# Normalising the sparse-attention probabilities inside the product that transposes them

## The chip, the cores and the metric

The kernel runs on one core of one Trainium2 chip. The metric is the device time of one launch in microseconds; the time before is the median of three runs. A core has a TensorE (PE, its weight loads shown apart as PEld), a VectorE (DVE), a ScalarE (ACT), a GpSimd (POOL) and a SyncE (SP). Each takes its own instructions in order; they wait for each other through semaphores.

## The reference, cut to what matters

Two transformer blocks follow one another on 512 tokens of width 1024. The change lies in the second block, in its sparse attention (16 heads, head size 64), whose two branches, "selected blocks" and "window", are both dense causal softmax attention at this length:

```python
s_s = jnp.einsum('bqghd,bgqkd->bgqhk', qb, k_g).astype(jnp.float32) * scale + group_bias(...)
p_s = masked_softmax(s_s, (dist_s >= 0)[:, :, :, None, :])
o_s = jnp.einsum('bgqhk,bgqkd->bqghd', p_s.astype(v_g.dtype), v_g)
...
out = gb[..., 0:1] * o_c + gb[..., 1:2] * o_s + gb[..., 2:3] * o_w
```

So each row of exponentials is divided by its sum and multiplied by a gate of the branch, and is then multiplied with the values.

## The kernel before

The kernel runs through block 1, then through a stage in which block 2 is projected, then through the stage `pa2` (opened in `emit`), then through the tail (mix, cross attention, feed-forward). In `pa2` three streams of work are woven by `weave`: the sparse attention (`nsa`, four groups of four heads, two branches each: 32 calls of `attend` with a gate), the RWKV recurrence (`rwkv_backs`, then `merge`, tiles with the suffix `_b` and `psn`) and a dense product for the gates (`merge_gates`, tiles `psg_m`). `attend` itself holds no yield, yet in the trace the instructions of the other streams stand between its own: the framework's planner lays out every engine's order when the kernel is compiled, by its own estimate of when each instruction is ready, and every engine then runs its list in that order.

One call of `attend` (L299 to L333) does this. For four blocks of 128 queries it multiplies queries with keys (L311, L312, into the PSUM tiles `psa`), adds the bias and takes the row minimum on DVE (L313), and takes the exponential and its row sum on ACT (L315). DVE takes the reciprocals of the four sums (L316) and multiplies them by the gate (L318). Then every probability tile is scaled in place by its row's reciprocal: the two wide ones (128x384 and 128x512) on ACT (L321), the two narrow ones on DVE (L323). After that, for four blocks of keys, PE transposes 4, 3, 2 and 1 squares of 128x128 (L328, ten in a call, into `psb`), ACT rounds the result (L330), DVE takes the remainder (L331), and two products with the values add up the output (L332, L333, into `pso`).

`attend` is called eight more times in block 1 without a gate. The transposes of a call are one instruction each: the moving operand is the identity, the stationary one is the probability square. The tile pool of `pa2` gives the key tiles (`kst`, pairs of high and low part) six buffers; `merge` later uses the same buffers for the operands of a product.

Of the kernel before, what the change touches and what calls it, by code (L numbers as in the profile page):

```python
# [11 lines left out]
AF = mybir.ActivationFunctionType  # L12
OP = mybir.AluOpType
# [25 lines left out]
class Gen:  # L39
# [259 lines left out]
    def attend(self, qst, kst, bias, V, o, first, last, gate=None):  # L299

        nc = self.nc
        kh, kl = kst
        st = self.f("sm", shape=(128, 32))
        m, s, r = st[:, 0:4], st[:, 4:8], st[:, 8:12]
        Pt = self.f("p", shape=(128, 1280))
        P = [Pt[:, 64 * i * (i + 1):64 * (i + 1) * (i + 2)] for i in range(4)]
        for i, pt in enumerate(P):
            w = 128 * (i + 1)
            ps = self.ps("a")
            qt = qst[:, i * 128:i * 128 + 128]  # L310
            nc.tensor.matmul(ps[:, :w], qt, kh[:, :w], start=True, stop=False)  # L311
            nc.tensor.matmul(ps[:, :w], qt, kl[:, :w], start=False, stop=True)  # L312
            nc.vector.tensor_tensor_reduce(pt, ps[:, :w], bias[:, 512 - w:], 1.0, 3e38, OP.add, OP.min,  # L313
                                           m[:, i:i + 1])
            nc.scalar.activation(pt, pt, AF.Exp, bias=m[:, i:i + 1], scale=-1.0, accum_out=s[:, i:i + 1])  # L315
        nc.vector.reciprocal(r, s)  # L316
        if gate is not None:
            nc.vector.tensor_tensor(r, r, gate, OP.mult)  # L318
        for i, pt in enumerate(P):
            if i >= 2:  # L320
                nc.scalar.activation(pt, pt, AF.Copy, scale=r[:, i:i + 1])  # L321
            else:
                nc.vector.tensor_scalar(pt, pt, r[:, i:i + 1], None, op0=OP.mult)  # L323
        for j in range(4):
            w = 512 - 128 * j
            ps = self.ps("b")
            for i in range(j, 4):
                nc.tensor.transpose(ps[:, (i - j) * 128:(i - j + 1) * 128], P[i][:, j * 128:j * 128 + 128], self.ident)  # L328
            ph, pl = self.f("pt", F32R), self.f("pt", F32R)
            nc.scalar.copy(ph[:, :w], ps[:, :w])  # L330
            nc.vector.tensor_tensor(pl[:, :w], ps[:, :w], ph[:, :w].bitcast(F32), OP.subtract)  # L331
            nc.tensor.matmul(o[:, j * 128:], V(j), ph[:, :w], start=first and j == 0, stop=False)  # L332
            nc.tensor.matmul(o[:, j * 128:], V(j), pl[:, :w], start=False, stop=last and j == 3)  # L333
# [903 lines left out]
    def merge(self, live):  # L1237

        nc, A, V = self.nc, self.A, self.nc.vector

        def first(n, g, p):
            self.mg.append(self.f("xh"))
            V.scalar_tensor_tensor(self.mg[n], g, 1.0, p, OP.add, OP.mult)

        def second(n, g, p):
            V.scalar_tensor_tensor(g, g, 1.0, p, OP.add, OP.mult)
            V.tensor_tensor(self.mg[n], self.mg[n], g, OP.add)

        def residual():
            x = self.x = [self.xtile(k, F32) for k in range(8)]  # L1250
            for k in range(8):
                nc.sync.dma_start(x[k], self.x2d[k])
            rs = self.bcast(self.colf)
            for k in range(8):
                V.scalar_tensor_tensor(x[k], x[k], self.vec("norm_final", k), rs, OP.mult, OP.mult)
                if "first" in self.dbg:
                    nc.sync.dma_start(self.dbg["first"][k * 128:(k + 1) * 128], x[k])
                yield 0.6
        while "_m" in live:
            yield None  # L1260
        self.mg = []
        load, product = self.branch(A["w_br_r"], self.yrd, 0, first,
                                    [("kb", 1024), ("y", 1024), ("vs", 1024), ("vu", 1024), ("bk", 1024), ("ys", 1024), ("as", 1024),
                                     ("y", 1024)], "vgb", "vgb")
        yield from load
        while "" in live and (w := next(product, None)) is not None:
            yield w
        while "" in live:
            yield None
        load, product_n = self.branch(A["w_br_n"], self.ynd, 8, second, ["kst"] * 3 + ["qst"] * 2 + ["pt"] * 2 + [("p", 1280)],  # L1270
                                      "f", "f")
        yield from self.side_by_side([product, load])
        yield from self.side_by_side([product_n, residual()])
# [169 lines left out]
def emit(tc, A, out, dbg={}):  # L1443
    nc = tc.nc
    with ExitStack() as ctx:
        g = Gen(tc, A, out, ctx)
        g.dbg = dbg
        scr = lambda n, s: setattr(g, n, nc.dram_tensor(n, s, F32, kind="Internal").ap())
        for n, s in dict(x2d=(8, 128, T), yrd=(8, 128, T), ynd=(8, 128, T), gtd=(128, T), gfd=(16, 1056),
                         grd=(16, 2, 640), adr=(4, 2, 4, 8, 32, 32), ydr=(4, 64, 32, 32), decd=(8, 128, 8), kbd=(8, 128, 1024),  # L1450
                         trd=(8, 128, 1024), tad=(8, 128, 1024), vgd=(8, 8, 128, T),
                         kvd=(8, 128, T), qd=(8, 128, T), vd=(2, 4, 128, 256), zmd=(16, 128, T),
                         ckd=(8, 128, 256), cvd=(2, 2, 128, T)).items():
            scr(n, s)
        g.setup()
        with g.phase("b1", act=16, f=3, sq=4, rs=3):
            xs = g.block1()
        g.banks = {"g": "01", "g_p": "23", "a": "45", "n": "6", "n_p": "7", "b": "67"}
        g.close_r()
        with g.phase("rec"):  # L1460
            g.rwkv_state()
            with g.phase("pa1", f=7, src_p=2, blk=2, cw=2, lt=3, kb=1, rkv=6, ar=1, cum=2, cx=1,
                         ys=1, f_p=4, cx_p=1, ws_p=2, wh_p=2, wl_p=2, **{"as": 1}):
                g.rwkv_consts()
                g.reserve(rkv=512, f=512, cum=520, cx=512, ar=1024, kb=1024, lt=1024, ys=1024, src_p=512, blk=1024,
                          cw=1024, cx_p=512, f_p=512, ws_p=1024, wh_p=1024, wl_p=1024, **{"as": 1024})
                g.run(g.rwkv_low(xs))

                def others():
                    yield from g.projections(xs)  # L1470
                    yield from g.merge_gates(xs, range(43, 49))
                g.weave(("", g.rwkv_fronts(xs), 245), ("_p", others(), 170))
            g.banks = {"a": "01", "b": "23", "n": "2", "o": "4", "a_b": "5", "b_b": "6", "g_m": "7", "g_b": "56"}
            g.side = nc.gpsimd
            with g.phase("pa2", f=3, ld=3, qst=5, kst=6, p=2, pt=4, bias=2, pc=2, kz=1, o=1, ot=1, vt=1,
                         kb=1, v=1, bk=1, ys=1, vs=2, vu=2, yc=6, vgb=2, y=2, f_m=1, **{"as": 1}):
                g.reserve(kb=1024, v=512, vs=1024, vu=1024, yc=128, bk=1024, y=1024, ys=1024,
                          vgb=512, ld=512, kst=512, vt=2048, qst=512, f=512, pc=512, bias=512)

                live = {"", "_m"}  # L1480

                def until(n, gen):
                    yield from gen
                    live.remove(n)

                def right():
                    yield from g.rwkv_backs()
                    yield from g.merge(live)
                g.weave(("", until("", g.nsa()), 190), ("_b", right(), 240), ("_m", until("_m", g.merge_gates(xs, range(49, 59))), 65))
            g.halves, g.side = None, nc.sync  # L1490
        g.banks = {"g": "01", "n": "2", "a": "34", "b": "56", "o": "7"}
        with g.phase("tail", act=52, f=16):
            g.mix()
            g.cross()
            g.ffn()
        g.close_r()
# [131 lines left out]
```

## Time and profile before

| what | us |
|---|---|
| median of three runs | 2083.45 (2080.49 to 2084.88) |
| profiled execution, its own time | 2082.19 |
| span of the profiled execution | 2080.4 |
| PE busy in the span | 2004.5 (96%) |
| DVE busy | 1308.6 (63%) |
| ACT busy | 925.3 (44%) |

The spans of the table are of one profiled execution; what lies around its span is 1.8 us. An instruction on PE is shown as a weight load (PEld) and a matmul; matmuls overlap each other, so a sum of their durations says more than the time that they cost, and the step from one start to the next is what counts. The 32 gated calls of `attend` lie between 1083 and 1450 us of the span.

### The profile page before, as it was taken

To read this page: it belongs to the slowest core of one execution; us is meant where nothing else is said; L and a number is where in the kernel's file an instruction comes from. 1 tells how busy PE (TensorE), PEld (TensorE's weight loads), DVE (VectorE), ACT (ScalarE), POOL (GpSimd) and SP (SyncE) were. 2 spreads that over 40 slices of the span, in tenths; PEclk is the share of its full clock that TensorE was granted. 3 is DMA by queue.
4 is the path that set the end of the run, shared out by engine and by line. 5 is a ranking of instruction groups with operands and counts; after the bars stand their busy time and mean duration, and the time that the engine had idled before them with its cause. 6 is when DMAs were issued, how large, how long until landed. Compare 5 with 4: busy or idle time off the path is not lost.

```text
span 2080.4 us, 27852 instructions
## 1 busy us (share of the span) xinstructions
PE 2004.5 (96%) x9927; PEld 1627.0 (78%) x9927; DVE 1308.6 (63%) x3007; ACT 925.3 (44%) x1778; POOL 95.5 (5%) x167
## 2 busy tenths in 40 slices
PE   8999999999999899899988899999999999999999
PEld 7778888888888677777767687887878778888887
DVE  5785432554463568687848988888466756666522
ACT  4874531442254233333346577777243443333311
POOL 0000000000003200000120111000000000000000
PEclk9999999999999999999989899999999999999999
DMA  5222332333355754755673445446442123333332
GB/s 161 82 85 93 99 93 92 117 108 120 117 185 158 171 147 141 183 147 168 191 168 105 129 122 145 126 123 190 154 140 84 41 81 92 101 92 98 95 109 84
DMA packets 178267, 256.75 MB, mean 123 GB/s; under 512 B 95409, under 2 KB 109953, under 8 KB 178129
## 3 DMA queue, kind: packets, MB, share of 16 engines
q1 hardware_dynamic: 162832, 231.31, 38.2%
q0 software_dynamic: 15296, 23.66, 3.9%
q8 instruction: 79, 1.29, 0.3%
q14 instruction: 60, 0.48, 0.1%
HBM read 205.12 MB, written 45.53 MB: 120 GB/s over the span
## 4 chain that ended last, share of the span: by engine, by line
PE 46%; DVE 6%; ACT 3%; issue 2%; DMA 2%; SPq 0%; POOL 0%; DVEq 0%; ACTq 0%; POOLq 0%
PE psg L243 8%; PE psg L245 8%; PE psg L244 8%; PE psg_b L243 1%; PE psg_b L244 1%; PE psg_b L245 1%; PE psb L328 1%; DVE ys L777 1%; PE psg_p L243 1%; PE psg_p L244 1%; PE psg_p L245 1%; PE pso L332 1%; PE psa L744 1%; DVE ys L778 1%; PE pso L333 1%
## 5 line engine op out<-in xcount | busy, mean ns | idle before, releaser
L222 ACT CAST wh<-ws 128x1024 fp32r<-128x1024 f32 (+2 forms) x283 | 291.6, 1031 | 697.9 <-PE psg L244 457.1
L223 DVE TENSOR_TENSOR wl<-ws,wh 128x1024 fp32r<-128x1024 f32 (+2 forms) x283 | 339.4, 1201 | 266.3 <-ACT wh L222 265.7
L243 PE MATMUL psg<-xh,wh 128*128 128x512 f32 x984 | 392.2, 399 | 4.7 <-ACT wh L222 4.7
L245 PE MATMUL psg<-xh,wl 128*128 128x512 f32 x984 | 393.1, 399 | 0.0
L244 PE MATMUL psg<-act,wh 128*128 128x512 f32 x912 | 359.7, 395 | 1.1 <-DVE act L166 1.1
L243 PEld LDWEIGHTS psg<-xh,wh 128*128 128x128 f32 x984 | 186.0, 189 | 46.8 <-ACT wh L222 5.5
L245 PEld LDWEIGHTS psg<-xh,wl 128*128 128x128 f32 x984 | 186.0, 189 | 41.5 <-issue 1.2
L244 PEld LDWEIGHTS psg<-act,wh 128*128 128x128 f32 x912 | 171.1, 188 | 42.8 <-DVE act L166 1.5
L243 PE MATMUL psg<-act,wh 128*128 128x512 f32 x496 | 196.1, 397 | 2.8 <-ACT act L165 1.4
L245 PE MATMUL psg<-act,wl 128*128 128x512 f32 x496 | 196.1, 396 | 0.5 <-DVE wl L223 0.5
L244 PE MATMUL psg<-xl,wh 128*128 128x512 f32 x352 | 139.7, 397 | 0.0
L243 PEld LDWEIGHTS psg<-act,wh 128*128 128x128 f32 x496 | 92.8, 188 | 27.2 <-ACT act L165 2.2
L245 PEld LDWEIGHTS psg<-act,wl 128*128 128x128 f32 x496 | 93.0, 187 | 23.7 <-DVE wl L223 1.3
L315 ACT ACTIVATE p<-p,sm 128x128 f32<-128x128 f32 (+3 forms) x160 | 89.6, 561 | 15.0 <-DVE sm L313 13.6
L331 DVE TENSOR_TENSOR pt<-psb,pt 128x512 fp32r<-128x512 f32 (+3 forms) x160 | 75.8, 487 | 20.0 <-ACT pt L330 17.7
L244 PE MATMUL psg<-x,wh 128*128 128x512 f32 x216 | 88.2, 409 | 0.0
L313 DVE CUSTOM_DVE_ANT_0 p<-psa,bias 128x128 f32<-128x128 f32 (+3 forms) x160 | 75.9, 485 | 8.2 <-PE psa L312 6.1
L328 PE MATMUL psb<-ident,p 128*128 128x128 f32 x400 | 75.3, 285 | 2.5 <-DVE y L921 0.9
L244 PEld LDWEIGHTS psg<-xl,wh 128*128 128x128 f32 x352 | 66.3, 188 | 14.0
L330 ACT CAST pt<-psb 128x512 fp32r<-128x512 f32 (+3 forms) x160 | 65.8, 424 | 25.7 <-PE psb L328 20.8
L243 PE MATMUL psg_p<-xh,wh 128*128 128x512 f32 x176 | 73.3, 416 | 1.1 <-ACT f L957 0.6
L244 PE MATMUL psg_p<-x,wh 128*128 128x512 f32 x176 | 72.2, 410 | 0.0
(491 smaller groups left out, 3899.1 us busy)
## 6 DMA issues: line engine op xcount, KB each, us to landing
ws<-in_w_in SPq DMA_DIRECT2D x49, 512.0 KB, 4.0
ws<-in_w_fup SPq DMA_DIRECT2D x44, 512.0 KB, 3.5
ws<-in_w_up SPq DMA_DIRECT2D x32, 512.0 KB, 3.5
ws<-in_w_down SPq DMA_DIRECT2D x32, 512.0 KB, 3.6
ws<-in_w_fdn SPq DMA_DIRECT2D x16, 512.0 KB, 3.6
ws<-in_w_qku SPq DMA_DIRECT2D x12, 512.0 KB, 3.6
ws<-in_w_in POOLq DMA_DIRECT2D x10, 512.0 KB, 4.6
ws<-in_w_out SPq DMA_DIRECT2D x8, 512.0 KB, 3.5
```

What stands on the lines that cost most here:

```text
L222: nc.scalar.copy(wh[:, :n], ws[:, :n])
L223: nc.vector.tensor_tensor(wl[:, :n], ws[:, :n], wh[:, :n].bitcast(F32), OP.subtract)
L243: nc.tensor.matmul(p[:, :n], wh[:, s], h[:, :n], start=c + k == 0, stop=False)
L244: nc.tensor.matmul(p[:, :n], wh[:, s], l[:, :n], start=False, stop=False)
L245: nc.tensor.matmul(p[:, :n], wl[:, s], h[:, :n], start=False, stop=last)
L313: nc.vector.tensor_tensor_reduce(pt, ps[:, :w], bias[:, 512 - w:], 1.0, 3e38, OP.add, OP.min, m[:, i:i + 1])
L315: nc.scalar.activation(pt, pt, AF.Exp, bias=m[:, i:i + 1], scale=-1.0, accum_out=s[:, i:i + 1])
L328: nc.tensor.transpose(ps[:, (i - j) * 128:(i - j + 1) * 128], P[i][:, j * 128:j * 128 + 128], self.ident)
L330: nc.scalar.copy(ph[:, :w], ps[:, :w])
L331: nc.vector.tensor_tensor(pl[:, :w], ps[:, :w], ph[:, :w].bitcast(F32), OP.subtract)
L332: nc.tensor.matmul(o[:, j * 128:], V(j), ph[:, :w], start=first and j == 0, stop=False)
L333: nc.tensor.matmul(o[:, j * 128:], V(j), pl[:, :w], start=False, stop=last and j == 3)
```

## The change

In gated calls the in-place scaling is dropped. Instead DVE builds, in one instruction, four diagonal squares in a new tile `dg` (128x512): the identity times the reciprocal of each row, once for each of the four query blocks. The transpose of a probability square is replaced by an ordinary fp32 matmul whose moving operand is the matching diagonal square. Calls without a gate keep the old form. To make room, `kst` has four buffers in `pa2` instead of six, and `dg` has two; `merge` takes a `dg` pair where it took the third `kst` pair.

```diff
-        for i, pt in enumerate(P):
-            if i >= 2:
-                nc.scalar.activation(pt, pt, AF.Copy, scale=r[:, i:i + 1])
-            else:
-                nc.vector.tensor_scalar(pt, pt, r[:, i:i + 1], None, op0=OP.mult)
+        if gate is not None:
+            dg = self.f("dg").rearrange("p (i n) -> p i n", i=4)
+            nc.vector.tensor_tensor(dg, self.ident[:, None, :].to_broadcast([128, 4, 128]),
+                                    r[:, :, None].to_broadcast([128, 4, 128]), OP.mult)
+        else:
+            dg = None
+            for i, pt in enumerate(P):
...
-                nc.tensor.transpose(ps[:, (i - j) * 128:(i - j + 1) * 128], P[i][:, j * 128:j * 128 + 128], self.ident)
+                src, dst = P[i][:, j * 128:j * 128 + 128], ps[:, (i - j) * 128:(i - j + 1) * 128]
+                if dg is not None:
+                    nc.tensor.matmul(dst, src, dg[:, i], start=True, stop=True)
+                else:
+                    nc.tensor.transpose(dst, src, self.ident)
...
-        ... ["kst"] * 3 + ["qst"] * 2 + ["pt"] * 2 + [("p", 1280)],
+        ... ["kst"] * 2 + ["dg"] + ["qst"] * 2 + ["pt"] * 2 + [("p", 1280)],
...
-            with g.phase("pa2", f=3, ld=3, qst=5, kst=6, p=2, ...
+            with g.phase("pa2", f=3, ld=3, qst=5, kst=4, dg=2, p=2, ...
```

## Rows read from the trace of the kernel before

**Rows 1.** The page, part 1: busy us, share of span, instructions.

```profile
span 2080.4 us, 27852 instructions
PE 2004.5 (96%) x9927; PEld 1627.0 (78%) x9927; DVE 1308.6 (63%) x3007; ACT 925.3 (44%) x1778; POOL 95.5 (5%) x167
```

**Rows 2.** Busy time of each engine by stretch, records in brackets.

```profile
core 0: us, PE busy (x) PEld busy (x) DVE busy (x) ACT busy (x) POOL busy (x), PEclk, DMA share, GB/s
1083.00:1200.00 117.00, 101.63 (x570) 83.66 (x569) 101.21 (x340) 73.92 (x212) 10.45 (x16) 0.88 0.46 118
1200.00:1410.00 210.00, 204.70 (x1294) 169.00 (x1293) 178.28 (x622) 161.29 (x460) 18.81 (x29) 1.00 0.48 130
1410.00:1450.00 40.00, 36.59 (x191) 28.57 (x191) 33.17 (x93) 31.59 (x76) 0.00 (x0) 0.96 0.59 187
1450.00:1500.00 50.00, 50.00 (x218) 40.23 (x217) 25.68 (x32) 11.34 (x13) 0.00 (x0) 1.00 0.50 154
```

**Rows 3.** Busy time of psg_m alone: PE, PEld, ACT (records), granted clock.

```profile
1200.00:1410.00 210.00, 52.08 (x148) 26.02 (x148) 3.57 (x6) 1.00 0.48 130
```

**Rows 4.** Chain that ended last, 1083 to 1447 us: shares by line.

```profile
by line: issue 8.0%; PE psb L328 7.0%; PE pso L332 5.3%; PE pso L333 3.9%; DMA kb<-kbd 3.6%; PE psa L311 3.5%; PE psb_b L888 3.2%; PE psb_b L891 3.0%; PE psa_b L879 3.0%; PE psa L312 2.9%; PE psb_b L874 2.9%; ACT p L315 2.7%; DVE pt L331 2.
```

**Rows 5.** Transposes (L328) and fp32 products of equal shape (L839): groups by shape.

```profile
L328 PE MATMUL psb<-ident,p 128*128 128x128 f32 x400 | 75.3, 285 | 2.5 <-DVE y L921 0.9 <-DVE p L323 0.7 <-ACT p L321 0.7
L839 PE MATMUL psa_b<-cen,v 128*128 128x128 f32 x64 | 10.1, 297 | 0.6 <-ACT wl L834 0.5
```

**Rows 6.** Timeline of PE: start us, length us, runs of L328, L839, 512-column products.

```profile
1305.73 0.82 PE L328 MATMUL psb<-ident,p 128*128 128x128 f32 x6
...
1355.00 1.16 PE L839 MATMUL psa_b<-cen,v 128*128 128x128 f32 x8
...
1411.26 0.39 PE L245 MATMUL psg_m<-xh,wl 128*128 128x512 f32 x1
...
1411.49 0.39 PE L243 MATMUL psg_m<-xh,wh 128*128 128x512 f32 x1
```

**Rows 7.** Busy time by stretch of L328 alone: PE, PEld (records), granted clock.

```profile
1083.00:1200.00 117.00, 17.14 (x87) 12.76 (x87) 0.88 0.46 118
1200.00:1410.00 210.00, 34.89 (x185) 23.25 (x185) 1.00 0.48 130
1410.00:1450.00 40.00, 8.50 (x49) 5.91 (x48) 0.96 0.59 187
```

**Rows 8.** Scaling on ACT by shape, 1083 to 1447 us: busy us, mean ns.

```profile
L321 ACT ACTIVATE p<-p,sm 128x512 f32<-128x512 f32 x32 | 22.8, 713 | 0.1
L321 ACT ACTIVATE p<-p,sm 128x384 f32<-128x384 f32 x32 | 19.6, 613 | 3.9 <-DVE sm L318 3.4
```

**Rows 9.** Timeline of DVE: one call's two scalings, start and length us.

```profile
1408.91 0.54 DVE L323 TENSOR_SCALAR p<-p,sm 128x128 f32<-128x128 f32 x2
```

**Rows 10.** DVE on 128x512 in SBUF; L1147 broadcasts one operand: ns min/median/max.

```profile
L1147 DVE TENSOR_TENSOR f<-f,sm x4: 679/683/690, 1078.5 to 1362.7; 128x512 f32<-128x512 f32 x4
...
L163 DVE TENSOR_TENSOR kst<-ld,kst x16: 661/688/696, 50.8 to 1349.2; 128x512 fp32r<-128x512 f32 x16
```

**Rows 11.** Who waited for whom, 1083 to 1447 us: total us, times, longest.

```profile
DVE pt L331 <- ACT pt L330: 14.5, 27, 1.2
ACT pt L330 <- PE psb L328: 14.3, 24, 1.9
...
PEld pso L332 <- ACT pt L330: 12.6, 41, 0.8
...
PEld psb L328 <- ACT p L321: 1.6, 5, 0.6
...
PEld psb L328 <- DVE p L323: 1.1, 3, 0.5
...
PE psb L328 <- ACT p L321: 0.7, 2, 0.4
```

**Rows 12.** Roundings of key tiles on ACT: ns min/median/max, first and last start.

```profile
L162 ACT CAST kst<-ld x16: 602/619/635, 50.2 to 1343.0; 128x512 fp32r<-128x512 f32 x16
```

More of the change, by code (lines that the diff above doesn't have):

```diff
@@ L318, in attend @@
             nc.vector.tensor_tensor(r, r, gate, OP.mult)
-        for i, pt in enumerate(P):
-            if i >= 2:
-                nc.scalar.activation(pt, pt, AF.Copy, scale=r[:, i:i + 1])
-            else:
-                nc.vector.tensor_scalar(pt, pt, r[:, i:i + 1], None, op0=OP.mult)
+        if gate is not None:
[5 more added lines that the diff above has]
+            for i, pt in enumerate(P):
+                if i >= 2:
+                    nc.scalar.activation(pt, pt, AF.Copy, scale=r[:, i:i + 1])
+                else:
+                    nc.vector.tensor_scalar(pt, pt, r[:, i:i + 1], None, op0=OP.mult)
         for j in range(4):
@@ L327, in attend @@
             for i in range(j, 4):
-                nc.tensor.transpose(ps[:, (i - j) * 128:(i - j + 1) * 128], P[i][:, j * 128:j * 128 + 128], self.ident)
+                src, dst = P[i][:, j * 128:j * 128 + 128], ps[:, (i - j) * 128:(i - j + 1) * 128]
+                if dg is not None:
+                    nc.tensor.matmul(dst, src, dg[:, i], start=True, stop=True)
+                else:
+                    nc.tensor.transpose(dst, src, self.ident)
             ph, pl = self.f("pt", F32R), self.f("pt", F32R)
@@ L1269, in merge @@
             yield None
-        load, product_n = self.branch(A["w_br_n"], self.ynd, 8, second, ["kst"] * 3 + ["qst"] * 2 + ["pt"] * 2 + [("p", 1280)],
+        load, product_n = self.branch(A["w_br_n"], self.ynd, 8, second, ["kst"] * 2 + ["dg"] + ["qst"] * 2 + ["pt"] * 2 + [("p", 1280)],
                                       "f", "f")
@@ L1474, in emit @@
             g.side = nc.gpsimd
-            with g.phase("pa2", f=3, ld=3, qst=5, kst=6, p=2, pt=4, bias=2, pc=2, kz=1, o=1, ot=1, vt=1,
+            with g.phase("pa2", f=3, ld=3, qst=5, kst=4, dg=2, p=2, pt=4, bias=2, pc=2, kz=1, o=1, ot=1, vt=1,
                          kb=1, v=1, bk=1, ys=1, vs=2, vu=2, yc=6, vgb=2, y=2, f_m=1, **{"as": 1}):
```

## The prediction

> **What bounds the kernel now.** I read the page first: over the whole span PE is busy 96%, DVE 63%, ACT 44% [rows 1]. That is an average over stages, and the change touches only the 32 gated calls between 1083 and 1450 us, so I cut that stretch in three [rows 2]. From 1083 to 1200 DVE is busy 101.2 of 117 us, PE 101.6 and at a granted clock of 0.88: neither engine is full, and the recurrence's triangular solves share DVE there. From 1200 to 1410 PE is busy 204.7 of 210 us, DVE 178.3 (85%) and ACT 161.3 (77%). From 1410 to 1450 all three have room. After 1450 PE is busy 50.0 of 50 us with dense products, so whatever end the stretch has, the rest is pushed back by as much.
>
> A busy PE is not a full PE. A matmul of 128 columns lasts 0.27 us but follows the one before it by 0.11, and one of 512 columns by 0.23 [rows 6]. The 1294 records of the middle stretch [rows 2] at 0.11 are 142 us, and the 148 of the dense product [rows 3] add 0.12 each, 18 us: at least 160 of 210 us are work. So PE has between 5 us (idle by the profile) and 50 us to spare there, in pieces mostly shorter than half a microsecond. The chain of waits over the stretch has the transposes as its largest single line, 7.0% of 364 us, which is 25.5 us [rows 4]; the ACT scaling is not among the lines that the view shows. So the likely bound is PE's own list, with DVE close behind it, and ACT third.
>
> **The change, part by part: PE.** Per call ten transposes become ten fp32 matmuls of the same shape. The trace has a sister of each. The transposes are 40 calls x 10 = 400 in the code and 400 records in the trace [rows 5]: one record each. L839 multiplies fp32 squares of the same shape; the code issues 8 x 4 = 32 of them and the trace has 64 records [rows 5]: two records each. Both kinds follow each other at about 0.11 us: six transposes take 0.82, (0.82 - 0.27) / 5 = 0.11; eight records of L839 take 1.16, (1.16 - 0.27) / 7 = 0.13 [rows 6]. So each replaced transpose costs PE one more step of 0.11 us: 320 x 0.11 = 35 us of new PE work, of which by the records [rows 7] 87 x 0.11 = 9.6 fall in the first stretch, 185 x 0.11 = 20.4 in the middle, 49 x 0.11 = 5.4 in the last.
>
> How much of it shows? At least nothing, at most all. The chain holds 25.5 us of transposes out of 320 x 0.11 = 35, so 72% by that reading; but a wait shorter than the 0.16 us by which records overlap is counted there as PE, so this leans high. I take a quarter in the first stretch (DVE is the busier there and PE waits, 2.4 us), 0.7 in the middle, near the chain's share (14.3), and 0.6 in the last, where a dense product fills part of the gaps (3.2): together +20 us.
>
> The Trainium skill (Perfetto Trace Analysis, Transposes) says that a logical transpose should be issued as a transpose and not as a standard matmul, because transposes skip the arithmetic. That speaks against this change, and the doubled records agree with its direction. The Trainium skill (TensorE: Matmul & The Clock Gate, Terms) goes further: its transpose mode is four times as fast for fp32, so by an estimate from that page a replaced transpose would cost three more steps, 320 x 0.33 = 106 us of PE work. The rows show two records, not four, and the sum goes by the rows.
>
> **DVE.** The two narrow scalings go: they overlap and take 0.54 us together [rows 9]. In comes one 128x512 product with both operands broadcast. The trace has none with two broadcasts; with one it takes 0.68, a plain split of that size 0.69 at the median [rows 10]. I take 0.68, so +0.14 a call, 4.5 us in 32 calls; none to 4.5 shows; with DVE at 85% I take a third, +1.5. If two broadcasts were slower by half, another 11 us would be DVE work and some 4 of it would show.
>
> **ACT.** The two wide scalings go: 22.8 + 19.6 = 42 us in 64 instructions [rows 8], ACT's share in the middle stretch falls from 77% to some 65%. Directly that is worth little: PE waited for ACT's scaling 1.6 + 0.7 us and for DVE's 1.1 [rows 11], and now it waits for `dg`, which comes 0.68 after the reciprocals, where the first scaled square came after 0.28 and the last after 0.61 + 0.71 = 1.3. The first four products then take 0.88 instead of 0.44, so the first rounding starts no sooner than before. Indirectly the roundings L330 stand in a shorter queue: PE waited 12.6 us for them and DVE 14.5 [rows 11]. At least nothing of these 27 us goes, at most all; I take 30%, -8 us, because ACT itself waits 14.3 us for the transposes that now take twice as long [rows 11].
>
> **Buffers and order.** With `kst` at four, the next group's keys are rounded and split only after the products of the last call that used the pair: 0.62 on ACT [rows 12] and 0.69 on DVE [rows 10], three handovers. A rounding that waits on ACT holds up the copies of the recurrence and the exponentials queued behind it, and PE behind those. One call lies between this release and the first use, which covers it, so nothing; without that cover 3 x 1.3 = 4 us. The key load waits in its `ld` buffer for that long, and the loads behind it on POOL's queue wait too; they are issued well ahead. `dg` has two buffers as the probabilities have, so its wait for a free one is theirs. In `merge` one pair of buffers has another name; nothing. The planner will lay out all lists anew, with either sign; PE's idle time by the profile is 15.4 + 5.3 + 3.4 = 24 us [rows 2], and I allow a quarter of it, 6 us, either way.
>
> **Sum.** 20 + 1.5 - 8 = +13.5 us. Against the profiled execution's own 2082.2 us (span 2080.4) this gives 2095.7; the median of the runs lies 1.3 above that execution, so I forecast 2097 us.
>
> **The rivals.** (1) ACT was the holder: its shorter queue lets the roundings come early, half of the 27 us of waits go (-13.5), and the new PE work falls into gaps but for some 4 us; about 2074 us, faster. It decides from the point at which less than a third of the 35 us shows. For it: 41 waits of PE for L330. Against it: no wait there is longer than 0.8 us, and the transposes feed those very roundings. (2) Gaps and relief cancel: PE has up to 50 us to spare in the middle stretch, 12 of the 35 us show, ACT gives back 8 to 12; about 2084, no difference. (3) All in series: 35 + 4.5 and no relief, 2123. For it: PE busy 204.7 of 210. Against it: DVE and ACT waits under those records. (4) The product with a diagonal square is one record like a transpose: no PE term, 1.5 - 8, 2077. L839 speaks against it. (5) Each replaced transpose takes four steps instead of one, as if L839's second record were two more: three times the PE term of the sum, 2083 + 60 - 6 = 2137. L839's two records at the plain step speak against it. This is what the Trainium skill's factor (TensorE: Matmul & The Clock Gate, Terms) would mean here.
>
> **How the numbers follow.** Forecast 0.55, rival 1 0.17, rival 2 0.17, rival 3 0.06, rival 4 0.03, rival 5 0.02. A measurement of this kernel tells about 0.2%, 4 us, from no change: 2079.3 to 2087.6 is the same. Faster 0.17 + 0.03 = 0.20, same 0.17, slower 0.55 + 0.06 + 0.02 = 0.63. The range reaches down to 2076, which takes in rivals 2 and 4 and the nearer half of rival 1, and up to 2114: the PE term at the chain's full share (+25), `dg` at its slow bound (+1.5 + 4), ACT's relief at 6 and the planner's 6 against us, 2083.4 + 30.5. Left out are half of rival 1, rivals 3 and 5 and little more, under 2 in 10. The forecast's own range is 2088 to 2110.
>
> **What would show it.** L328 in gated calls should have 640 records instead of 320 at the same step; if 320, rival 4 holds. `dg` should show 32 instructions of about 0.68 us. ACT's busy time should fall by some 40 us and PE's waits for L330 below 12.6. The distance from the first gated call to the end of the last should grow by some 13 us, most of it between 1200 and 1410; if PE's busy share there stays near 97% while the stretch grows, PE is the bound; if PE's idle time falls by as much as its work rises, rival 2 holds. Wrong would be the share that shows: it is the term that no row gives.

## The result

The changed kernel takes 2111.59 us (median of 4 runs, 2108.06 to 2115.3) where the kernel before takes 2081.97 (4 runs): the ratio is 1.0143, with a 95% interval of 1.0123 to 1.0163. That is 29.6 us slower. The profiled execution took 2110.2 us. All differences in us below are (ratio − 1) x 2083.

The page of the changed kernel, part 1: busy time, share of the span, instructions.

```profile
span 2108.4 us, 28411 instructions
...
PE 2038.0 (97%) x10247; PEld 1666.2 (79%) x10247; DVE 1313.6 (62%) x2975; ACT 891.8 (42%) x1714; POOL 95.1 (5%) x167
```

Beside [rows 1], PE has 320 records and 33.5 us of busy time more, ACT 33.5 us less, DVE 5.0 more. PE's idle time, span less busy, fell from 75.9 to 70.4 us. So PE's gaps took up little of its new work, and the time that ACT lost does not come off the span.

The stretch of the gated calls in the changed kernel, cut as in [rows 2] with the last two cuts moved by 28 us (busy time of each engine, records in brackets, granted clock).

```profile
core 0: us, PE busy (x) PEld busy (x) DVE busy (x) ACT busy (x) POOL busy (x), PEclk, DMA share, GB/s
1083.00:1200.00 117.00, 107.43 (x666) 91.79 (x665) 101.97 (x331) 64.28 (x196) 10.48 (x16) 0.91 0.44 117
1200.00:1410.00 210.00, 202.56 (x1335) 174.16 (x1335) 164.31 (x550) 126.28 (x376) 17.82 (x28) 0.99 0.44 118
1410.00:1478.00 68.00, 64.78 (x374) 53.55 (x374) 52.99 (x147) 42.51 (x109) 0.78 (x1) 0.95 0.52 160
1478.00:1528.00 50.00, 50.00 (x219) 40.17 (x218) 24.10 (x29) 10.56 (x11) 0.00 (x0) 1.00 0.44 137
```

The same stretches for the products with the diagonal alone (L336, which stands for the gated calls of L328): PE, PEld, granted clock.

```profile
1083.00:1200.00 117.00, 25.94 (x174) 24.97 (x174) 0.91 0.44 117
1200.00:1410.00 210.00, 47.47 (x334) 44.12 (x334) 0.99 0.44 118
1410.00:1478.00 68.00, 20.80 (x132) 18.96 (x132) 0.95 0.52 160
```

Two records make a square. By 1200 us the changed kernel has done 174 / 2 = 87 squares, as many as before (87, [rows 7]): in this profile the first stretch costs nothing that can be seen. Between 1200 and 1410 it does 167 where the kernel before does 185. PE's other records in that stretch lag too: 1335 − 334 = 1001 against 1294 − 185 = 1109. At 1410 it is 18 squares behind; the kernel before needs 210 / 185 = 1.135 us for one, so that is 20 us. The last gated call ends 27.6 us later than before, so the last stretch adds some 7. PE's busy share in the middle stretch is 96.5%, where it was 97.5%, while everything in it was spread out. Behind the gated calls nothing changed: from their end to the end of the kernel it takes 631.9 us, before 631.5. (In the other runs this rest takes 630 to 638 us.)

The products themselves in the changed kernel: first their group (records, busy us, mean ns, idle before), then two runs of them in PE's timeline (start, length, in brackets the idle time before).

```profile
L336 PE MATMUL psb<-dg,p 128*128 128x128 f32 x640 | 94.2, 284 | 0.8 <-DVE dg L321 0.4 <-DVE y L931 0.4
```

```profile
1206.56 1.80 PE L336 MATMUL psb<-dg,p 128*128 128x128 f32 x14 [0.40 <-DVE dg L321]
...
1301.85 1.72 PE L336 MATMUL psb<-dg,p 128*128 128x128 f32 x14
```

There are 640 records for 320 squares, and they follow each other at (1.72 − 0.27) / 13 = 0.11 us, the step of the transposes in [rows 6].

The chain that ended last in the changed kernel, 1083 to 1478 us, by line.

```profile
by line: PE psb L336 14.3%; PE pso L342 5.2%; PE pso L343 5.0%; issue 4.2%; PE psb_b L898 4.0%; PE psa L311 3.6%; PE psa L312 3.4%; PE psb_b L884 3.4%; PE psa_b L889 3.4%; PE psb_b L901 3.1%; DMA kb<-kbd 2.9%; PE pso L1198 2.6%; PE psg_m L2
```

L336 holds 14.3% of 395 us, 56 us, where the transposes held 25.5 [rows 4]: +31, nearly as much as PE's busy time rose.

The waits of the changed kernel in that stretch: who waited for whom, total us, times, longest.

```profile
ACT pt L340 <- PE psb L336: 42.0, 53, 4.7
...
DVE pt L341 <- ACT pt L340: 23.4, 31, 3.1
...
PEld pso L342 <- ACT pt L340: 9.1, 19, 2.8
...
PEld pso L343 <- DVE pt L341: 7.1, 21, 1.3
...
PE pso L342 <- ACT pt L340: 4.6, 5, 2.5
...
ACT kst L162 <- PE psa L311: 1.2, 2, 0.7
```

L340 is the rounding that was L330, L341 the remainder that was L331, L342 and L343 the products that were L332 and L333. ACT now waits for the squares 42.0 us instead of 14.3, and DVE waits for the rounding 23.4 instead of 14.5 [rows 11]. PE still waits for the rounding about as long as before: 9.1 + 4.6 us, where it was 12.6 + 1.5 (the 1.5 is shown with e7 below).

### The profile page after: what moved, and what is told of

It reads as the page before. It is cut to its first block, busy times and chain, and to the rows that moved or that the text cites. A ratio compares the mean times of both kernels' runs of the same rounds, so it can differ in the third digit from the quotient of the medians.

```text
span 2108.4 us, 28411 instructions
## 1 busy us (share of the span) xinstructions
PE 2038.0 (97%) x10247; PEld 1666.2 (79%) x10247; DVE 1313.6 (62%) x2975; ACT 891.8 (42%) x1714; POOL 95.1 (5%) x167
## 4 chain that ended last, share of the span: by engine, by line
PE 48%; DVE 5%; DMA 3%; ACT 2%; issue 1%; SPq 0%; POOL 0%; DVEq 0%; ACTq 0%; POOLq 0%
PE psg L245 8%; PE psg L243 8%; PE psg L244 8%; PE psb L336 3%; PE psg_b L243 1%; PE psg_b L245 1%; PE psg_b L244 1%; PE pso L342 1%; DVE ys L787 1%; PE psg_p L244 1%; PE psg_p L243 1%; PE psg_p L245 1%; PE pso L343 1%; PE psa L754 1%; PE psb_b L898 1%
## 5 line engine op out<-in xcount | busy, mean ns | idle before, releaser
L336 PE MATMUL psb<-dg,p 128*128 128x128 f32 x640 | 94.2, 284 | 0.8 <-DVE dg L321 0.4
L341 DVE TENSOR_TENSOR pt<-psb,pt 128x512 fp32r<-128x512 f32 (+3 forms) x160 | 74.8, 487 | 30.0 <-ACT pt L340 26.1
L336 PEld LDWEIGHTS psb<-dg,p 128*128 128x128 f32 x640 | 88.0, 199 | 5.4 <-issue 1.3
L340 ACT CAST pt<-psb 128x512 fp32r<-128x512 f32 (+3 forms) x160 | 66.0, 425 | 54.1 <-PE psb L336 42.0
L244 PEld LDWEIGHTS psg<-xl,wh 128*128 128x128 f32 x352 | 66.2, 188 | 14.3
```

The lines of the kernel that those rows point to most:

```text
L244: nc.tensor.matmul(p[:, :n], wh[:, s], l[:, :n], start=False, stop=False)
L336: nc.tensor.matmul(dst, src, dg[:, i], start=True, stop=True)
```

## The experiments

The theory to be tested was that of the prediction with a larger share: the second record of each square is paid almost in full, and ACT's relief gives little back. Against it stood that the loss comes from something else that the change brings: the build of `dg` and the wait for it, the two key buffers that went, or the order that the planner lays out anew.

**The second record alone (e1, e4).** e1 takes the kernel before and makes each gated transpose a product with the identity; the scaling stays.

```
-  nc.tensor.transpose(ps[...], P[i][...], self.ident)
+  if gate is not None:
+      nc.tensor.matmul(ps[...], P[i][...], self.ident, start=True, stop=True)
+  else:
+      nc.tensor.transpose(ps[...], P[i][...], self.ident)
```

> The kernel before, scaling on ACT and DVE kept, but the ten transposes of each gated call are ordinary fp32 matmuls by the identity: only PE's part of the change. Theory A (PE's list is the bound, and taking the scaling off ACT gave nothing): the whole loss of 28 us is here, before + 25 to 33 us, 2107 to 2115. Theory B (PE's part is about the +20 of the forecast, and the rest of the loss comes from the wait for dg on DVE): before + 15 to 21, 2097 to 2103. L328 in gated calls has 640 records under both.

Measured: 1.0074 [1.0054, 1.0094], +15 us. The group of L329 in e1:

```profile
L329 PE MATMUL psb<-ident,p 128*128 128x128 f32 x640 | 96.5, 286 | 1.1 <-DVE p L323 0.6 <-ACT p L321 0.2
```

e4 issues each gated transpose of the kernel before twice, so that it has as many records without any true fp32 product.

```
+  for _ in range(1 if gate is None else 2):
       nc.tensor.transpose(ps[...], P[i][...], self.ident)
```

> The kernel before, each transpose of a gated call issued twice into the same place: two records per square as the fp32 product has, with no fp32 arithmetic. If the number of records is what costs: within 4 us of e1, about 2107 to 2115. If the arithmetic of the product costs something of its own (a longer step, slower loads): e1 is slower than this by 6 us or more.

Measured: 1.0111 [1.0086, 1.0137], +23 us. The group of L329 in e4 (640 records of gated calls, 80 of others):

```profile
L329 PE MATMUL psb<-ident,p 128*128 128x128 f32 x720 | 108.8, 281 | 1.7 <-DVE p L323 1.4
```

L329 alone by stretch, first in e1, then in e4 (PE and PEld busy, records, granted clock):

```profile
1083.00:1200.00 117.00, 28.64 (x180) 26.92 (x180) 0.93 0.46 124
1200.00:1410.00 210.00, 48.09 (x332) 44.52 (x332) 0.98 0.44 117
```

```profile
1083.00:1200.00 117.00, 24.82 (x162) 21.32 (x162) 0.88 0.43 108
1200.00:1410.00 210.00, 48.72 (x346) 40.06 (x346) 1.00 0.48 126
```

By 1200 us e1 has done 90 squares and e4 81, where the kernel before and the changed one have done 87. By 1410 they have done 256 and 254, where it is 272 before and 254 in the changed kernel: with records doubled and nothing else changed, either is as far behind there as the changed kernel is. Where on the way the lag arises differs from order to order.

The record lasts as long as in e1 (281 and 286 ns), and the loss is no smaller. So doubling the records is enough to cost as much, whatever is computed in them. The two together, which have the same records, put the price of the second records, added to the kernel before, at about 20 us of the 35. What they cost within the changed kernel is another question (e7 and e8). The 8 us between them are no more than the order alone can make (e9 and e10 below).

**The relief alone (e2).** The kernel before without the scaling of gated calls; their probabilities stay unnormalised.

```
-  for i, pt in enumerate(P):
+  for i, pt in enumerate(P if gate is None else []):
```

> The kernel before without the scaling in gated calls (the probabilities stay unnormalised; reciprocals and gate product are still formed but not applied), transposes kept: what taking 64 instructions off ACT and 64 off DVE is worth. Theory A: 0 to 4 us less, 2078 to 2082. The forecast's term: 8 us less or a little more with DVE's share, 2072 to 2075. Rival 1 of the forecast (ACT holds the stage): 13 us less or more, under 2069.

Measured: 0.997 [0.9956, 0.9984], −6 us. The page of e2, part 1:

```profile
span 2078.2 us, 27693 instructions
...
PE 2000.7 (96%) x9927; PEld 1625.5 (78%) x9927; DVE 1293.7 (62%) x2943; ACT 888.7 (43%) x1714; POOL 95.4 (5%) x167
```

ACT loses 36.6 us of work against [rows 1] and DVE 14.9, and the kernel gains 6. That is what taking the scaling away brings in the kernel before, under the order that this one version got, with nothing put in its place. ACT's wait for the squares, from the waits of e2 between 1083 and 1443 us and of e6 (below) between 1083 and 1452:

```profile
ACT pt L330 <- PE psb L328: 29.6, 37, 3.4
```

```profile
ACT pt L330 <- PE psb L328: 27.5, 30, 3.5
```

In both the squares are plain transposes, and still ACT waits for them about twice as long as the 14.3 us of [rows 11]: with the scaling gone, it comes to the rounding earlier and waits there for PE.

**The buffers (e5), and the relief with the buffers cut (e6).** e5 is the kernel before with the change's buffers; `dg` is there and nobody writes it in the gated calls. e6 is e2 with the same edit.

```
-  ["kst"] * 3 + ["qst"] * 2 + ...
+  ["kst"] * 2 + ["dg"] + ["qst"] * 2 + ...
-  ... qst=5, kst=6, p=2, ...
+  ... qst=5, kst=4, dg=2, p=2, ...
```

> The kernel before with the change's buffers alone: kst with four buffers in the place of six, dg reserved but unused until merge takes it; scaling and transposes as before. Theory K (the cut of the key buffers is what e3 lost against e2: the next group's keys are split late): before + 8 to 16 us, 2095 to 2103 where before gives 2087. Theory D (the dg instruction on DVE, in the row's critical place, is what e3 lost): within 4 us of before.

Measured: 1.0018 [1.0005, 1.0031], +4 us.

> e2 with the change's buffers (kst four, dg reserved, not built); so e3 without its 32 dg instructions (probabilities unnormalised). Theory K: as e3, some 10 us over before, 16 over e2. Theory D: as e2, some 6 us under before. If it lies halfway, both take part.

Measured: 1.0022 [1.0009, 1.0035], +5 us. With the buffers cut, the 6 us of e2 are gone: against e5, which has the same buffers, taking the scaling away brings nothing (+5 and +4). The changed kernel's only direct sign of the cut is the last line of the waits above, ACT's rounding of keys waiting 1.2 us for the score products that still read the buffer.

**`dg` built but not used (e3).** The changed kernel with the transposes put back; the probabilities stay unnormalised. It differs from e6 by the 32 builds of `dg`, which nobody waits for.

```
-  nc.tensor.matmul(dst, src, dg[:, i], start=True, stop=True)
+  nc.tensor.transpose(dst, src, self.ident)
```

> The changed kernel with transposes by the identity in place of the products: dg is built on DVE but nobody reads it (the probabilities stay unnormalised), and kst has four buffers. Against e2 it adds the 32 dg instructions and the cut of the buffers. Theory A: within 4 us of e2, 2078 to 2084. Theory B: dg on DVE and the buffers cost 5 us or more over e2.

Measured: 1.0047 [1.0029, 1.0064], +10 us, 5 more than e6. From here to the changed kernel, which adds the second records and the wait for `dg`, there are 20 us more.

**No wait for one's own `dg` (e8).** The changed kernel, whose products read the diagonal of the call before; the normalisation is then that of another call.

```
   nc.vector.tensor_tensor(dg, self.ident[...], r[...], OP.mult)
+  dg, self.dg = self.dg or dg, dg
```

> The changed kernel, but each call's products read the diagonal that the call before built (the probabilities are normalised by the wrong call's reciprocals), so no product waits for its own dg; the same instructions otherwise. If the wait for dg is what the change lost beyond e3 (which has transposes and no wait): some 12 us under the change, before + 15 to 20. If the fp32 product itself is (its records, its place in PE's list): within 4 us of the change, before + 26 to 32.

Measured: 1.01 [1.0067, 1.0132], +21 us, 9 less than the changed kernel and 11 more than e3. That lies between the two expectations. What the wait itself was in the changed kernel, by the view of one line (L321, the build of `dg`): durations in ns as minimum, median and maximum, first and last start, and who waited for it.

```profile
L321 DVE TENSOR_TENSOR dg<-ident,sm x32: 673/686/693, 1085.1 to 1469.7; 128x512 f32<-128x512 f32 x32
...
who waited for it (us, times):
  PEld psb L336: 0.9, 4
  PE psb L336: 0.4, 1
```

The waits for `dg` sum to 1.3 us, so they do not make 9 us by themselves. And ACT waits for the squares in e8 (L337 there) almost as long as in the changed kernel:

```profile
ACT pt L341 <- PE psb L337: 40.0, 50, 1.9
```

So e8 doesn't show that the wait for `dg` costs 9 us; another order laid out for another list of dependencies may do as well. L337 alone by stretch in e8:

```profile
1083.00:1200.00 117.00, 30.23 (x180) 26.77 (x178) 0.91 0.46 117
1200.00:1410.00 210.00, 57.96 (x352) 50.48 (x352) 1.00 0.45 121
```

With two records for every square e8 has done 266 squares by 1410 us, only 6 fewer than the kernel before; e1, e4 and the changed kernel are 16 to 18 behind there.

**One record per square (e7).** The changed kernel with `p` and `dg` rounded to fp32r and the product in that type.

```
-  dg = self.f("dg")...
+  dg = self.f("dg", F32R)...
-  nc.tensor.matmul(dst, src, dg[:, i], start=True, stop=True)
+  nc.tensor.matmul(dst, src.bitcast(F32R), dg[:, i], start=True, stop=True)
```

The exponentials and the step before them write `pt.bitcast(F32R)` in gated calls.

> The changed kernel with the product by the diagonal in the short fp32r form, which takes one record per square like a transpose (scores, probabilities and diagonals are rounded to that form, so the result is coarser); dg, its wait and four kst buffers as in the change. Theory A or D/K alike: it lacks the 320 second records, so it is 12 to 20 us faster than the change and stands near e3, before + 8 to 14. If PE's records were not what the product costs, it would stand near the change, before + 25 or more. If K or D were wrong and only records cost, it would be at before - 6.

Measured: 1.0104 [1.0078, 1.0131], +22 us. The group of L336 in e7:

```profile
L336 PE MATMUL psb<-dg,p 128*128 128x128 f32 x320 | 52.9, 273 | 0.8 <-DVE dg L321 0.4 <-DVE y L931 0.4
```

The second records are gone and still 22 of the 30 us remain. That is 8 less than the changed kernel, where 12 to 20 were expected. This speaks against the theory that the records are all. The waits of e7 between 1083 and 1478 us:

```profile
PEld pso L342 <- ACT pt L340: 22.5, 39, 3.4
...
PE pso L342 <- ACT pt L340: 13.8, 17, 3.1
PEld pso L343 <- DVE pt L341: 13.5, 29, 2.8
PE pso L343 <- DVE pt L341: 6.2, 8, 2.5
```

The value products wait 22.5 + 13.8 + 13.5 + 6.2 = 56 us for the rounded squares. In the kernel before the same four waits are 12.6 + 1.5 + 5.8 + 1.8 = 22 us (1083 to 1447 us; the first of them is in [rows 11], the others here):

```profile
PEld pso L333 <- DVE pt L331: 5.8, 17, 1.7
PE pso L333 <- DVE pt L331: 1.8, 3, 1.4
...
PE pso L332 <- ACT pt L330: 1.5, 4, 0.6
```

Most of these waits lie under other records of PE. The page of e7, part 1, and its stretch from 1410 to 1450 us:

```profile
PE 2015.7 (96%) x9927; PEld 1635.1 (78%) x9927; DVE 1313.3 (63%) x2975; ACT 889.2 (42%) x1714; POOL 95.1 (5%) x167
```

```profile
1410.00:1450.00 40.00, 35.06 (x167) 27.76 (x168) 28.38 (x90) 22.95 (x62) 0.78 (x1) 0.83 0.54 171
```

The span of e7 is 2100.3 us, 19.9 longer than before. PE's idle time makes 8.7 of it (84.6 instead of 75.9), and PE's busy time, with the same 9927 records, the other 11.2. Between 1410 and 1450 us PE is busy 35.1 of 40 us at a mean granted clock of 0.83, where before it was 36.6 at 0.96 [rows 2]. Why e7's order puts the value products so near behind the roundings is not settled.

Set against e3, which also has `dg`, four key buffers and one record a square, e7 has products that need `dg` in the place of transposes (and rounded probabilities and diagonals), and it is 12 us slower. That points the same way as e8, which lacks this dependency and is 9 us faster than the changed kernel. Read along this path, the loss is 10 us for e3, 9 to 12 for the dependency on `dg`, and only 8 (e7 to the changed kernel) to 11 (e3 to e8) for the second records, where e1 and e4 have 15 and 23. Each step is within what order alone makes, so neither reading is shown.

**The order alone (e9 to e12).** Each edit so far also makes the planner lay out all lists anew. To size that, the rate of the attention's list in the planner's weave goes from 190 to 186 and to 194, in the kernel before (e9, e10) and in the changed kernel (e11, e12). No instruction that counts as busy is added or taken away.

```
-  g.weave(("", until("", g.nsa()), 190), ("_b", right(), 240), ...
+  g.weave(("", until("", g.nsa()), 186), ("_b", right(), 240), ...
```

> The kernel before with one number of the weave changed (the attention stream's rate 190 to 186): the same work, another order from the planner. What a mere new laying-out of the lists costs or gains. If differences between the experiments of 4 to 8 us are chance of the order: this moves by as much, either way. If orders are alike in worth: within 2 us of before.

Measured: 1.0006 [0.9987, 1.0025], +1 us.

> As e9 with the rate at 194, the other way: a second draw of the same chance. Same bounds: beyond 4 us from before shows that the order alone can make such a difference; within 2 us shows that it does not.

Measured: 1.0062 [1.0042, 1.0083], +13 us. The page of e10, part 1:

```profile
span 2096.5 us, 27848 instructions
...
PE 2013.2 (96%) x9927; PEld 1630.7 (78%) x9927; DVE 1308.0 (62%) x3007; ACT 924.2 (44%) x1778; POOL 95.4 (5%) x167
```

Every engine has the same number of busy instructions as in [rows 1], DVE and ACT have the same busy time within 1.1 us, and yet the span is 16 us longer. Order alone does that. It does so in two ways: PE is idle for 7.4 us more (83.3 instead of 75.9), and the same 9927 records keep it busy for 8.7 us more, at a mean granted clock of 0.977 over the span where the kernel before has 0.981.

> The changed kernel with the weave's rate for the attention at 186. Beside e9 it gives a second pair of changed and unchanged kernel under another order. If the loss is the change's own: 20 to 35 us over e9, so 2105 to 2120 where before gives 2086. If a good part of the 30 us was the draw of the order: under 15 us over e9.

Measured: 1.0117 [1.0102, 1.0132], +24 us; over e9, its partner at the same rate, +23.

> The changed kernel with the rate at 194, beside e10 (which lost 13 us by the order alone). If the loss is the change's own and adds to the order's: 33 to 48 over before, 2119 to 2134. If the change's lists do not share the bad order of e10: 20 to 35 over before, 2106 to 2121.

Measured: 1.0157 [1.014, 1.0174], +33 us; over e10 +20.

So the change costs +30, +23 and +20 us in three pairs, 24 us on the mean: the kernel before lies at 0, +1 and +13, the changed one at +30, +24 and +33. The loss is the change's own. Of the 30 us measured some 6 may belong to the layout that this one version happened to get.

No version tried beats the kernel before with all of its computation in it; e2 is faster only without the normalisation.

## Why the prediction was right or wrong

The sign was right, and so was the bound as far as the traces tell: between 1200 and 1410 us PE stays 96.5% busy while its stretch grows, and new PE work shows there. The size, +13.5, was less than half of what came. The 2111.6 us lie above the forecast's own range (2088 to 2110) and within the wide one only near its upper end of 2114, which was reached by letting four terms go wrong at once. They went wrong otherwise than the sum to 2114 has it: ACT's relief did not shrink by 2 us but vanished. That the time still fell inside is partly luck. Step by step:

**Two records a square, at 0.11 us.** Right. There are 640 records at that step, and PE's busy time rose by 33.5 us against 35 in the sum. With this rival 4 (one record) falls, and rival 5 too. The Trainium skill (TensorE: Matmul & The Clock Gate, Terms) gives its transpose mode four times the speed for fp32; here the factor is two records to one. Its rule that a transpose should be issued as one (the Trainium skill, Perfetto Trace Analysis, Transposes) holds in e1, at +15 us for 320 squares; e4 adds that by these rows the count of records is enough to explain it.

**The share that shows.** The sum took 2.4 us in the first stretch and 14.3 in the middle, 16.7 by 1410 us. The profiles have e1, e4 and the changed kernel 16 to 18 squares behind there, 18 to 20 us at 1.135 us each: about right. How it divides between the first two stretches no single profile settles (87, 90 and 81 squares by 1200). In the last stretch the sum had 3.2 us, and the changed kernel loses some 7, with everything else that the change brings in it. As a whole the term's +20 agrees with e1 and e4 (15 and 23), but not with the steps that end or begin at e7 and e8 (8 and 11); that these 18 to 20 us come from the second records alone is therefore not shown for the changed kernel.

**ACT's relief, −8.** This is the term of the sum that failed most. Taking the scaling away brings 6 us in e2, but with the buffers cut as the change cuts them nothing is left of it (e6, +5). The step said that 30% of the 27 us of waits for and behind the roundings would go, because their queue is shorter. In the changed kernel these waits are 9.1 + 4.6 for PE and 23.4 for DVE, 37 us instead of 29 (the 27 and the 1.5 that the 27 left out), and ACT's own wait for PE is 42.0 instead of 14.3. ACT's busy time fell by 33.5 us, but ACT spends the time gained waiting for the squares, and it does so with plain transposes too (29.6 us in e2, 27.5 in e6). The prediction named that wait and still took a relief.

**`dg`.** 0.686 us was measured where 0.68 was taken; DVE's busy time rose by 5.0 us against 4.5. The waits for it are 1.3 us. Between e6 and e3 its 32 builds cost 5 us where +1.5 stood in the sum, but 5 us is within what order makes. That the products need `dg` stood at nothing in the sum; e8 and e7 point to 9 to 12 us, which is not shown.

**Buffers, 0 with 4 as the bound.** e5 gives +4 [1, 6], the bound itself. The direct wait is 1.2 us.

**Planner's order, ±6, not in the sum.** Too narrow for what a new order can do: the re-laid kernel before (e9, e10) moves by +1 and by +13. Nothing in the trace of one order gives that size; it takes a second order to see it.

**The rivals.** Rivals 1 and 2 needed ACT to give back 8 to 14 us or the new work to fall into gaps; e2 and e6 (6 us less and nothing) refute the first, and PE's idle time, which fell by 5.5 us only, the second. Rival 3, all in series at 2123, is 11 us above the measurement; against it stands that no run shows the 35 us in full (e1 15, e4 23).

What remains open is how the loss divides. That it is the change's own, 20 to 30 us in three pairs, is shown; that second records cost time when they are added to the kernel before is shown too (e1, e4), and that no relief of 8 us came. One sum takes about 20 us for the second records and 4 for the buffers, 24 as the three pairs have on the mean; it leaves e7 unexplained, which lacks the second records and loses 22 us all the same. Another takes e3's 10, some 10 for the dependency on `dg` and some 10 for the second records. Both are argued, not shown: each edit re-lays the order, and that alone moves the time by up to 13 us. It would take e7 and e8 built at several rates of the weave to part them.

## What to carry to other kernels

Folding a scaling into a transposing product moves work from the vector engines to TensorE, and here, in fp32, it doubled TensorE's records for the transposes. In a stretch in which TensorE was 97% busy this did not pay; whether it pays where TensorE has idle time was not tried. Work taken off an engine that waits for TensorE brought almost nothing: 51 us off ACT and DVE were worth 6, and nothing once the buffers were cut. Where a planner lays out the order, re-lay the unchanged kernel once or twice with a slightly different rate before reading a difference; here that moved the time by up to 13 us, more than e2, e3, e5 and e6 did. And build the changed kernel again too: the three pairs tell more than any single edit.

## What the runs showed of the hardware

A wait of PE can be followed by a slower clock, so that order may cost twice. In e3 the granted clock fell to half right behind a stretch in which PE was less busy (busy time by stretch, records in brackets, then the granted clock):

```profile
1262.00:1272.00 10.00, 9.96 (x71) 8.49 (x70) 8.65 (x37) 5.68 (x18) 0.00 (x0) 1.00 0.54 132
1272.00:1282.00 10.00, 7.27 (x41) 5.15 (x39) 7.25 (x21) 4.08 (x9) 1.39 (x2) 0.99 0.75 206
1282.00:1299.00 17.00, 14.23 (x55) 12.34 (x56) 8.51 (x23) 9.45 (x30) 2.18 (x4) 0.50 0.31 96
1299.00:1310.00 11.00, 10.94 (x68) 9.05 (x68) 9.86 (x34) 6.93 (x22) 0.82 (x1) 1.00 0.25 69
```

Between 1272 and 1282 us PE was busy 7.27 of 10 us, and for the 17 us behind it the clock was at 1.2 GHz, the lower of its two levels: 55 records, 3.2 per us, where the stretches on either side did 7.1 and 6.2. Then it came back. What this one stretch cost is not measured; in e10 and e7, with as many records as before, PE's busy time rose by 8.7 and 11.2 us. Such stretches alone do not sort the kernels by time, though: between 1083 and 1200 us e9 has a mean clock of 0.85 where the kernel before has 0.88 [rows 2], and it takes the same time (+1 us).
